# A list schedule on every queue from the out-projection's tenth tile to the ConvGLU's fourth unit

## Chip, cores and metric

The kernel runs on one core of one Trainium2 chip. Its time is the device time of one execution, in microseconds (us); the figures below are single executions and their median.

## What is computed

One hybrid decoder layer over 16 meta tokens and 512 tokens, with model width 2048, a hidden width of 5632 in the gated feed-forward part, all in fp32. Cut to its frame:

```python
h = jnp.concatenate([meta, x], axis=1)
n = rmsnorm(h, g_pre_mix)
z = n @ w_in
y_conv = short_conv_group(z[..., :CONV_COLS], conv_w)
y_rwkv = rwkv7_group(z[..., CONV_COLS:], ...)          # a scan over the tokens, 16 heads of 64
h = h + rmsnorm(jnp.concatenate([y_conv, y_rwkv], -1) @ w_out, g_post_mix)
gate, up = jnp.split(rmsnorm(h, g_pre_ffn) @ w_gate_up, 2, axis=-1)
h = h + rmsnorm((silu(causal_dwconv(gate, conv_ffn)) * up) @ w_down, g_post_ffn)
return h[:, N_META:]
```

## The kernel before

Features lie on the partitions and tokens along the free axis. KT = 16 blocks of 128 features make the model width. Tokens go in two halves of 258 and 256 columns (HY, lines 558 on; the two columns more are what the convolution looks back on). Every product of matrices is made of three fp32r matmuls: each operand is split in a high part (hi, cast by ScalarE, ACT) and a low part (lo, subtracted by VectorE, DVE), and hi by hi, hi by lo and lo by hi are summed in PSUM. In the rows `whi`, `wlo`, `H`, `O` and `tt` are split weights, `ahi` and `alo` are split activations, `R` and `raw` are the buffers into which weights land.

Work goes in three stages.

**Mixer (about 20 to 740 us).** The in-projection and the scan. Its instructions are not issued as written: class `Plan` (line 222) keeps them, estimates a duration for each (`time`) and a landing time for each DMA (`land`), and sorts each engine's queue by a list schedule with ranks (`order`, `run`). `give` (line 466) then issues them in that order under a manual schedule. A DMA's landing is taken as the issue, plus its bytes over 230 KB a us, plus LAND = 1.2 us, plus 2 us more if it has 4*NC = 68 partitions. A matmul of the rank FILL = 9 goes where nothing of a better rank is ready. The scan passes its matrices through DRAM: small tiles `Pi` go out to `d` (16 transfers of 32 partitions), a tile `tb` of 68 partitions goes out to `d`, and `AT` is read back from `d` in 32 transfers of 32 partitions. Its rounds are matmuls `st<-x,AT`, followed by `SUV` on DVE, ACT and GpSimd (POOL), before the next round's matmul.

**Out-projection and residual (about 740 to 1030 us).** Thirteen of the 16 output blocks of `w_out` (loop `for m in range(KT - 3)`, with `gemm`) are done for both token halves at a time. The last three are done by halves: first the three blocks' half 0 with the split weights kept in `tt0` to `tt2`, then the three blocks' half 1. Meanwhile `mixed` squares the outputs and sums the squares in `ss`, and copies them to `acc`. When half 0 is complete, `rms2` makes its norm (a ones-matmul into `psn`, then a few instructions on DVE and ACT that leave the factor `r1` in SBUF, in the tile `hxl`). `residual(i)` then takes blocks two at a time, eight pairs for each half: `xT` is loaded into one of three `q` buffers, DVE multiplies `acc` by `r1`, POOL adds `xT`, ACT and DVE split the sum to `ahi` and `alo`. The first units' matmuls (f = 0 and 1, half 0 and half 1, functions `halves2` and `standard`) read these.

PE's order here is the order of the code (a manual schedule for PE, line 1270), with `residual`'s steps started at fixed counts N1 = 9 and N2 = 5. The other queues are ordered by the framework's own scheduler.

**ConvGLU (to the end).** 44 units of 128 hidden features. Units f = 0 to 3 are plain products. From f = 4 on a unit is seven products of half size (`seven`), each one a "unit" of the list `units`, with sums of weights (DVE, POOL) and sums of activations (`X1` to `X4`, made once by `sums` and `last_sum`). After each group of four f, `down` adds the product with `w_down`. The list is issued with the products in order (line 1678). At the end come the second norm and the output.

Of the kernel before, what the change touches and what calls it, by code (L numbers as in the profile page):

```python
# [76 lines left out]
N4 = 2  # L77

# [117 lines left out]
class Pool:  # L196
# [3 lines left out]
    def tile(self, shape, dtype, **kw):  # L200
        if not self.plan.on:
            return self.real.tile(shape, dtype, **kw)
        t = Tile(self, shape, dtype, kw)
        return View(t, (), shape[0], t.ids)
# [17 lines left out]
class Plan:  # L222
# [243 lines left out]
    def give(self):  # L466
        self.on = False
        with self.tc.manual_schedule():
            for x in self.order():
                getattr(x["engine"], x["op"])(*x["args"], **x["kw"])  # L470
        self.kept = []


def hymba(tc, I, out, ysp=None):
# [60 lines left out]

    def split(x, hi, lo, scale=None):
# [18 lines left out]
    def rms(ss, r, m, q, psp, tag, pb=2, eps=None):  # L555
# [12 lines left out]
        V.tensor_tensor(out=r, in0=r, in1=q, op=ALU.mult)  # L568
# [621 lines left out]
    with tc.tile_pool(name="p2", bufs=1) as p2, tc.tile_pool(name="ps2", bufs=1, space=PSUM) as ps2:  # L1190
# [18 lines left out]
        def rms2(ss, r):  # L1209

            n = r.shape[-1]
            m = small(n)
            rms(ss, r, m, small(n), ps2, "d")
            return m

# [10 lines left out]
        def mixed(ps, m, i):  # L1226
# [3 lines left out]
            S.activation(out=sq[i], in_=x, func=AF.Square)  # L1230
# [4 lines left out]
        def residual(i, b12):  # L1235
# [3 lines left out]
            for m in range(0, KT, 2):  # L1239
                xr = two()[:, :, :b - a]  # L1240
# [10 lines left out]
        def act(b12, m, i):  # L1251

            if i and m < KT // 2:
                return [b12[:, m, p] for p in range(2)]
            return [x[:, i * HA:i * HA + 258] for x in hs[m]]
# [14 lines left out]
        with tc.manual_schedule(engines={mybir.EngineType.PE}):  # L1270
            last = []
            for n, m in enumerate(range(KT - 3, KT)):
                kw = p2.tile([128, KT // 4, 2, 512], F32R, name=f"tt{n}", bufs=1)
                keep = [(kw[:, ku, 0], kw[:, ku, 1]) for ku in range(KT // 4)]
                if n == 0:
                    ps = [ps2.tile([128, 512], F32, name="u", bufs=2) for _ in range(2)]
                else:
                    t = mp.tile([128, 2, 512], F32, name="mps")
                    ps = [t[:, i] for i in range(2)]
                run(gemm(I["w_out"][m], ys, half(ps, 0), into=keep))  # L1280
                mixed(ps, m, 0)
                last.append((ps, keep))
            n = 0
            res = iter(())
            for m, (ps, keep) in zip(range(KT - 3, KT), last):
                for _ in gemm(None, ys, half(ps, 1), kept=keep):
                    n += 1
                    if n == N1:
                        rms2([ss[0], sq[0]], r1[0])
                        res = residual(0, None)  # L1290
                    if n % 4 == 0:
                        next(res, None)
                mixed(ps, m, 1)
            run(res)


            H = KT // 2

            def block(n):
                return p2.tile([128, H, 2, 258], F32R, name=f"tt{n}", bufs=1)  # L1300

            b12 = block(2)
            rb = wide("rb")
            rw = [rb[:, i * HW:i * HW + 258] for i in range(2)]

            def load(src):
                raw = big("R", F32)
                SP.dma_start(raw, src)
                return raw

            def parted(raw, hi=None, lo=None):

                hi, lo = hi or [big("H")], lo or [big("O")]
                n = 1024 // len(hi)
                for i, x in enumerate(hi):
                    S.copy(x, raw[:, i * n:i * n + n])
                n = 1024 // len(lo)
                for i, x in enumerate(lo):
                    hn = len(hi) * n // 1024
                    hp = hi[0][:, i * n:i * n + n] if len(hi) == 1 else hi[i]  # L1320
                    V.tensor_tensor(out=x, in0=raw[:, i * n:i * n + n], in1=hp.bitcast(F32), op=ALU.subtract)

                def at(parts, c):
                    n = 1024 // len(parts)
                    return parts[c // n][:, c % n:c % n + 128]
                return lambda c: at(hi, c), lambda c: at(lo, c)

            def standard(outs, w, m0, x, first, last):

                for j in range(KT // 2):  # L1330
                    for pi, (p, q) in enumerate(((0, 0), (0, 1), (1, 0))):
                        for o, i, c in outs:
                            PE.matmul(o, w[p](128 * j), x(m0 + j, i)[q][:, c:258], start=(first and j == 0 and pi == 0),
                                      stop=(last and j == KT // 2 - 1 and pi == 2))
                    yield

            def x_of(m, i):
                return act(b12, m, i)
# [3 lines left out]
            hid = {}  # L1342

            def chain(f, zg, up, i0=0, i1=2, s=None):


                s = {} if s is None else s
                z3 = zg.rearrange("p (i t) -> p i t", i=2)[:, i0:i1]
                r3 = rb.rearrange("p (i t) -> p i t", i=2)[:, i0:i1]
                w = slice(256 * i0, 256 * i1)  # L1350

                def half3(x):
                    return x[:, w].rearrange("p (i t) -> p i t", t=256)

                def c0():
                    G.tensor_tensor(out=z3[:, :, :258], in0=z3[:, :, :258], in1=r3[:, :, :258], op=ALU.mult)

                def c1():
                    if "u" not in s:
                        s["u"] = wide()  # L1360
                    S.activation(out=half3(s["u"]), in_=z3[:, :, 0:256], func=AF.Copy, scale=pc("conv_ffn", f))

                def c2():
                    u3 = half3(s["u"])
                    for i in (1, 2):
                        V.scalar_tensor_tensor(out=u3, in0=z3[:, :, i:i + 256], scalar=pc("conv_ffn", i * NF + f),
                                               in1=u3, op0=ALU.mult, op1=ALU.add)

                def c3():
                    u = s["u"]  # L1370
                    S.activation(out=u[:, w], in_=u[:, w], func=AF.Silu)
                    if isinstance(up, list):
                        for i in range(2):
                            o = u[:, 256 * i:256 * i + 256]
                            V.tensor_tensor(out=o, in0=o, in1=up[i], op=ALU.mult)
                    else:
                        V.tensor_tensor(out=u[:, w], in0=u[:, w], in1=up[:, w], op=ALU.mult)

                def c4():
                    if f not in hid:  # L1380
                        if f % GF < 3:
                            hid[f] = [wp.tile([128, 512], F32R, name=n, bufs=3) for n in ("whi", "wlo")]
                        else:
                            hid[f] = [p2.tile([128, 2 * HW], F32R, name=n, bufs=1)[:, :SEQ] for n in ("hxh", "hxl")]
                    split(s["u"][:, w], *[x[:, w] for x in hid[f]])

                return [c0, c1, c2, c3, c4]

            def plain(f, ps, pu):
                zg = wide()  # L1390
                for i in range(2):
                    S.copy(zg[:, i * HW:i * HW + 258], ps[i])
                return chain(f, zg, pu)

            def first(f, n):
                t = mp.tile([128, 2, 512], F32, name="mps")
                u = ps2.tile([128, 512], F32, name="u", bufs=2)
# [463 lines left out]
```

## Time and profile before

| | us |
|---|---|
| three executions | 2421.02, 2416.26, 2418.2 |
| median | 2418.2 |
| the profiled execution | 2420.04 |
| its span on the core | 2417.9 |

| engine | busy us | share of the span | instructions |
|---|---|---|---|
| PE (matmul) | 2365.9 | 98% | 18546 |
| DVE | 1700.5 | 70% | 2274 |
| ACT | 1195.3 | 49% | 2343 |
| POOL | 670.8 | 28% | 753 |

Busy PE is not PE at its full rate: the profile also gives the clock that TensorE was granted, 1.0 being 2.4 GHz and 0.5 being 1.2 GHz. Over the whole span it is 0.994. A row such as "PE mps <- DVE alo: 6.0, 1, 6.0" says that PE, ahead of a matmul into `mps`, stood idle 6.0 us in total, once, until a DVE instruction that wrote `alo` released it.

### The profile page before, as it was taken

The numbers are of one execution on the slowest core, as the hardware profiler recorded it, in microseconds if no ns is written. First come the engines' busy times: TensorE is split into PE (matmuls) and PEld (weight loads), VectorE is DVE, ScalarE is ACT, GpSimd is POOL, SyncE is SP. The second block draws the span as 40 slices with busy tenths as digits, with TensorE's granted clock in tenths as the row PEclk, the third lists the DMA queues.
The fourth block names the chain that finished last, engine by engine and source line by source line (L and its number), as shares of the span: only waits on it lengthen the run. The fifth ranks groups of instructions, "written<-read, shape, count | busy, mean of one in ns | idle before, by whom it ended". The sixth has DMA issues, their size and how long they took to land.

```text
span 2417.9 us, 46262 instructions
## 1 busy us (share of the span) xinstructions
PE 2365.9 (98%) x18546; PEld 2253.1 (93%) x18546; DVE 1700.5 (70%) x2274; ACT 1195.3 (49%) x2343; POOL 670.8 (28%) x753
## 2 busy tenths in 40 slices
PE   7999999999999999999999999999999999999996
PEld 7999999999999999898999999999989898989896
DVE  7677888978754523885767777686868685859586
ACT  7756766666653533464434434343434252525254
POOL 2222747456350011531212111121212120202025
PEclk9999999999999999999999999999999999999998
DMA  5443333333433633523242424232424242323252
GB/s 180 146 140 107 93 89 88 103 106 87 136 98 92 201 92 110 175 66 97 82 127 79 131 79 123 81 121 77 126 68 140 70 131 79 119 83 108 94 194 73
DMA packets 130103, 265.53 MB, mean 110 GB/s; under 512 B 29888, under 2 KB 42944, under 8 KB 129888
## 3 DMA queue, kind: packets, MB, share of 16 engines
q1 hardware_dynamic: 129888, 262.57, 35.6%
q8 instruction: 146, 2.39, 0.4%
q14 instruction: 69, 0.57, 0.1%
HBM read 239.57 MB, written 22.95 MB: 109 GB/s over the span
## 4 chain that ended last, share of the span: by engine, by line
PE 90%; DVE 5%; DMA 2%; issue 1%; ACT 1%; POOL 0%; SPq 0%; DVEq 0%; ACTq 0%; POOLq 0%
PE mps L218 58%; PE u L218 16%; PE d L218 10%; PE st L218 4%; PE aux L218 2%; DVE acc L218 1%; DMA raw<-w_in_dram 1%; DVE raw L218 1%; DVE q L218 0%; DVE O L218 0%; DVE alo L218 0%; DVE tt L218 0%; DVE wlo L218 0%; DMA d<-tb 0%; DMA AT<-d 0%
## 5 line engine op out<-in xcount | busy, mean ns | idle before, releaser
L218 ACT CAST H<-R 128x1024 fp32r<-128x1024 f32 x373 | 391.9, 1051 | 454.8 <-PE u L218 177.6
L218 DVE TENSOR_TENSOR O<-R,H 128x1024 fp32r<-128x1024 f32 x373 | 488.9, 1311 | 109.0 <-ACT H L218 108.8
L218 PE MATMUL mps<-ahi,whi 128*128 128x264 f32 (+2 forms) x2048 | 411.2, 289 | 10.2 <-ACT whi L218 10.0
L218 PE MATMUL mps<-ahi,wlo 128*128 128x258 f32 (+2 forms) x2048 | 409.6, 288 | 1.6 <-DVE wlo L218 1.6
L218 PE MATMUL mps<-alo,whi 128*128 128x264 f32 (+2 forms) x2048 | 407.7, 287 | 0.2 <-DVE alo L218 0.2
L218 DVE TENSOR_TENSOR wlo<-raw,whi 128x512 fp32r<-128x512 f32 x289 | 209.1, 727 | 209.3 <-ACT whi L218 194.8
L218 PEld LDWEIGHTS mps<-ahi,whi 128*128 128x128 f32 x2048 | 313.5, 190 | 13.0 <-ACT whi L218 10.1
L218 PEld LDWEIGHTS mps<-ahi,wlo 128*128 128x128 f32 x2048 | 313.9, 190 | 4.3 <-DVE wlo L218 1.8
L218 PEld LDWEIGHTS mps<-alo,whi 128*128 128x128 f32 x2048 | 312.8, 190 | 2.2 <-DVE alo L218 0.5
L218 ACT CAST whi<-raw 128x512 fp32r<-128x512 f32 x289 | 178.3, 620 | 201.0 <-PE mps L218 154.4
L218 POOL TENSOR_TENSOR raw<-raw,rb 128x516 f32<-128x516 f32 (+1 forms) x45 | 92.5, 2057 | 627.8 <-DVE raw L218 613.1
L218 PE MATMUL mps<-tt,H 128*128 128x258 f32 x1968 | 263.3, 284 | 1.8 <-ACT q L218 1.8
L218 PE MATMUL mps<-alo,H 128*128 128x258 f32 x1032 | 255.2, 284 | 6.0 <-DVE alo L218 6.0
L218 PE MATMUL mps<-ahi,H 128*128 128x258 f32 x1032 | 255.1, 284 | 1.1 <-ACT q L218 1.1
L218 PEld LDWEIGHTS mps<-tt,H 128*128 128x128 f32 x1968 | 249.2, 190 | 2.0 <-ACT q L218 2.0
L218 POOL TENSOR_TENSOR R<-R 128x1024 f32<-128x1024 f32 x40 | 133.4, 3334 | 422.1 <-DVE R L218 422.1
L218 DVE TENSOR_TENSOR R<-R 128x1024 f32<-128x1024 f32 x120 | 208.9, 1741 | 1.1
L218 PEld LDWEIGHTS mps<-alo,H 128*128 128x128 f32 x1032 | 194.8, 190 | 6.7 <-DVE alo L218 6.2
L218 PEld LDWEIGHTS mps<-ahi,H 128*128 128x128 f32 x1032 | 195.4, 190 | 1.8 <-ACT q L218 1.3
L218 POOL TENSOR_SCALAR SUV<-VT 32x64 f32<-32x64 f32 x272 | 144.3, 531 | 137.0 <-PE st L218 109.7
L218 PE MATMUL mps<-ahi,O 128*128 128x258 f32 x1032 | 153.5, 284 | 0.0
L218 PE MATMUL mps<-tt,O 128*128 128x258 f32 x984 | 141.8, 283 | 0.0
(319 smaller groups left out, 4478.0 us busy)
## 6 DMA issues: line engine op xcount, KB each, us to landing
R<-w_gu_dram SPq DMA_DIRECT2D x176, 512.0 KB, 3.6
raw<-w_in_dram SPq DMA_DIRECT2D x208, 256.0 KB, 2.7
R<-w_down_dram SPq DMA_DIRECT2D x88, 512.0 KB, 4.4
raw<-w_out_dram SPq DMA_DIRECT2D x64, 256.0 KB, 2.7
l<-lo SPq DMA_DIRECT2D x24, 264.0 KB, 2.2
hsp<-acc SPq DMA_DIRECT2D x8, 512.0 KB
tt<-hsp SPq DMA_DIRECT2D x4, 1024.0 KB, 11.1
lo<-l SPq DMA_DIRECT2D x12, 264.0 KB, 3.5
```

Source lines behind the costliest of these rows:

```text
L218: return getattr(self.real, op)(*real, **{k: x.get() if isinstance(x, View) else x for k, x in kw.items()})
```

## The change

The plan that orders the mixer is used again, from the out-projection's block M0 = 10 to the ConvGLU's list entry K0 = 4, for all queues. Around that the code is changed as follows.

- Only the last two blocks of `w_out` are done by halves, not three.
- `rms1` writes the factor r1 into a PSUM tile, `r1p`. `residual` loads `xT` into a `raw` buffer (ring of three), multiplies by `r1p`, and adds on POOL and DVE in turn.
- Half 0's split blocks 0 to 7 get a block of their own, `b11` (tile `tt2`), from which `X11` is later read; half 1's go to the first columns of `hs`. `X4` then takes the place of those and needs no block.
- The sums of squares are added on DVE alone. `sums` and `last_sum` scale `h` on ACT (`normed`) and subtract pairs of blocks on DVE (`less`).
- `land` adds its 2 us also to transfers of C = 32 partitions, and Silu has a number in the table of ACT's function sets. Both bear on the mixer's order too, as all `d<-Pi` and `AT<-d` transfers have 32 partitions.
- All matmuls are the same ones, in another order.

```diff
-        return self.pipe + LAND + (2.0 if a.parts == 4 * NC else 0)
-    TABLE = {AF.Exp: 1, AF.Sigmoid: 2, AF.Tanh: 2, AF.Abs_reciprocal_sqrt: 3}
+        return self.pipe + LAND + (2.0 if a.parts in (C, 4 * NC) else 0)
+    TABLE = {AF.Exp: 1, AF.Sigmoid: 2, AF.Tanh: 2, AF.Abs_reciprocal_sqrt: 3, AF.Silu: 4}
...
+    def fill(g):
+        g = iter(g)
+        while True:
+            with plan.step(2, FILL):
+                try:
+                    next(g)
+                except StopIteration:
+                    return
+            yield
...
+        def rms1(i):
+            o = ps2.tile([128, 512], F32, name="r1p", tag="d", bufs=2)[:, :HY[i][1] - HY[i][0]]
+            with plan.step(0):
+                rms2([ss[i], sq[i]], r1[i], o)
+            r1[i] = o
...
-                xr = two()[:, :, :b - a]
+                xr = wide().rearrange("p (m t) -> p m t", m=2)[:, :, :b - a]
...
-                G.tensor_tensor(out=x, in0=x, in1=xr, op=ALU.add)
+                (G if m % 4 else V).tensor_tensor(out=x, in0=x, in1=xr, op=ALU.add)
                 for n in (m, m + 1):
-                    split(h[:, n, c:d], *act(b12, n, i), pc("g_ffn", n))
+                    with plan.step(1):
+                        split(h[:, n, c:d], *act(n, i), pc("g_ffn", n))
...
-        for m in range(KT - 3):
+        for m in range(KT - 2):
+            plan.on = m >= M0
...
-            run(gemm(I["w_out"][m], ys, [half(ps, i)[0] for i in range(2)]))
+            run(fill(gemm(I["w_out"][m], ys, [half(ps, i)[0] for i in range(2)])))
...
+        for k in range(-6, K0):
+            with plan.step(2, FILL):
+                if k >= 0:
+                    units[k][1]()
+            with plan.step(2):
+                if k > 0:
+                    units[k - 1][2]()
+                for e in ev.pop(k, []):
+                    e()
+                if 0 <= k + 2 < len(units):
+                    units[k + 2][0]()
+        plan.give()
```

Three places show what moves. The first is DVE's queue behind half 0's norm, before; `psn` is the sum of squares, `acc,hxl` the multiplication by r1, `tt<-R` the low parts of unit 1's weights, `alo` those of the activations:

```order
L218 TENSOR_SCALAR q<-psn 128x258
L218 TENSOR_TENSOR q<-q 128x258
L218 TENSOR_SCALAR q<-q 128x258
L218 TENSOR_TENSOR hxl<-hxl,q 128x258
L218 TENSOR_TENSOR acc<-acc,hxl 128x2x258 x8
L218 TENSOR_TENSOR tt_13691<-R,tt_13691 128x1024 x2
L218 TENSOR_TENSOR tt_13700<-R,tt_13700 128x1024 x2
L218 SCALAR_TENSOR_TENSOR alo_11511<-acc,par,ahi_11510 128x258
```

The same place of DVE's queue in the changed kernel, where `tt_13584` is the own block for half 0 and `acc,raw` the addition of `xT`:

```order
L220 TENSOR_SCALAR q<-psn 128x258
L220 TENSOR_TENSOR q<-q 128x258
L220 TENSOR_SCALAR q<-q 128x258
L220 TENSOR_TENSOR r1p<-hxl,q 128x258
L220 TENSOR_TENSOR acc<-acc,r1p 128x2x258 x4
L220 TENSOR_TENSOR acc<-acc,raw 128x2x258
L220 SCALAR_TENSOR_TENSOR tt_13584<-acc,par,tt_13584 128x258 x4
L220 TENSOR_TENSOR acc<-acc,raw 128x2x258
L220 TENSOR_TENSOR acc<-acc,r1p 128x2x258
L220 SCALAR_TENSOR_TENSOR tt_13584<-acc,par,tt_13584 128x258
```

Behind four multiplications and one addition come the first four low parts; the weights' low parts (`tt<-R`) have moved behind half 1's.

The second is ACT's queue where the first products of unit 4 end, before; `q<-mps` copies a finished product out of PSUM, `tt<-raw` is the high part of a late sum:

```order
L218 CAST tt_14713<-raw 128x2x258 x3
L218 CAST H<-R 128x1024
L218 COPY raw<-mps 128x258 x2
L218 CAST H<-R 128x1024
L218 COPY q<-mps 128x258
L218 ACTIVATE raw<-raw,par 128x512
L218 CAST tt_14713<-raw 128x258
L218 CAST H<-R 128x1024
L218 COPY q<-mps 128x258
L218 CAST tt_14713<-raw 128x258
L218 CAST H<-R 128x1024
L218 COPY q<-mps 128x258
```

In the changed kernel the late sums are `ahi_...<-raw`:

```order
L220 COPY raw<-mps 128x258 x2
L220 ACTIVATE q<-acc,par 128x258 x2
L220 CAST H<-R 128x1024
L220 CAST ahi_13883<-raw 128x258
L220 CAST ahi_13888<-raw 128x258
L220 CAST H<-R 128x1024
L220 COPY q<-mps 128x258
L220 ACTIVATE raw<-raw,par 128x512
L220 ACTIVATE q<-acc,par 128x258
L220 CAST H<-R 128x1024
L220 CAST ahi_13832<-raw 128x258
L220 COPY q<-mps 128x258
```

The first copy stands behind two casts of sums that were subtracted earlier; of the later two, one has a cast of a late sum ahead of it instead of both.

The third is SyncE's queue, SP, in the mixer, at the scan's third set of matrices, before; `d_...<-tb` sends them out and `AT<-d` reads them back:

```order
L218 DMA d_7045<-tb 68x1024
L218 DMA ysp<-sg 128x514
L218 DMA raw<-w_in_dram 128x512
L218 DMA sg<-l_1606 128x528
L218 DMA raw<-w_in_dram 128x512
L218 DMA AT<-d_7045 32x9x32 x4
L218 DMA AT<-d_7045 32x8x32 x2
L218 DMA raw<-w_in_dram 128x512
L218 DMA AT<-d_7045 32x8x32 x2
```

And in the changed kernel:

```order
L220 DMA ysp<-sg 128x514
L220 DMA raw<-w_in_dram 128x512 x2
L220 DMA sg<-l_1606 128x528
L220 DMA d_7113<-tb 68x1024
L220 DMA raw<-w_in_dram 128x512 x2
L220 DMA AT<-d_7113 32x9x32 x4
L220 DMA AT<-d_7113 32x8x32 x4
```

The store of y and the load of `sg` no longer stand between the sending and the reading back, and the eight readings go in one row.

## Rows read from the trace of the kernel before

**Rows 1.** The page's parts 1 and 4: engines, and the chain that ended last.

```profile
PE 2365.9 (98%) x18546; PEld 2253.1 (93%) x18546; DVE 1700.5 (70%) x2274; ACT 1195.3 (49%) x2343; POOL 670.8 (28%) x753
...
PE 90%; DVE 5%; DMA 2%; issue 1%; ACT 1%; POOL 0%; SPq 0%; DVEq 0%; ACTq 0%; POOLq 0%
```

**Rows 2.** PE's waits, 650 to 1250 us: us in total, times, longest.

```profile
PE mps L218 <- DVE alo L218: 6.0, 1, 6.0
PE mps L218 <- ACT q L218: 2.9, 2, 1.8
PE u L218 <- DVE raw L218: 0.4, 1, 0.4
```

**Rows 3.** Windows: us, each engine's busy time (instructions), PEclk, DMA share, GB/s.

```profile
960.00:970.00 10.00, 10.00 (x85) 10.00 (x85) 0.69 (x1) 2.06 (x6) 1.65 (x2) 1.00 0.01 2
...
980.00:990.00 10.00, 8.00 (x67) 7.79 (x65) 10.00 (x7) 6.88 (x15) 8.82 (x7) 1.00 0.49 114
990.00:1000.00 10.00, 6.00 (x31) 5.78 (x32) 8.75 (x16) 1.93 (x6) 5.23 (x3) 0.66 0.71 257
...
1100.00:1110.00 10.00, 7.12 (x47) 6.71 (x47) 8.24 (x14) 6.41 (x11) 0.00 (x0) 0.86 0.46 150
1110.00:1120.00 10.00, 10.00 (x69) 9.41 (x69) 5.39 (x8) 3.99 (x6) 2.15 (x1) 0.97 0.66 218
```

**Rows 4.** The chain that ended last, 980 to 1000 us: start, us, what.

```profile
979.58 7.90 DVE acc L218 x5
...
988.54 5.00 DVE tt L218 x3
993.55 0.41 DVE alo L218
```

**Rows 5.** DVE's instructions by shape, 972 to 994 us: busy us, mean ns, idle before.

```profile
L218 DVE TENSOR_TENSOR acc<-acc,hxl 128x516 f32<-128x516 f32 x8 | 10.9, 1433 | 0.0
L218 DVE TENSOR_TENSOR tt<-R,tt 128x1024 fp32r<-128x1024 f32 x4 | 6.1, 1592 | 0.0
L218 DVE SCALAR_TENSOR_TENSOR alo<-acc,par,ahi 128x258 fp32r<-128x258 f32 x2 | 0.9, 477 | 0.0
L218 DVE TENSOR_SCALAR q<-psn 128x258 f32<-128x258 f32 x1 | 0.4, 428 | 12.8 <-PE psn L218 12.8
```

**Rows 6.** DVE and POOL by shape, 972 to 1107 us.

```profile
L218 DVE SCALAR_TENSOR_TENSOR alo<-acc,par,ahi 128x258 fp32r<-128x258 f32 x24 | 13.7, 635 | 0.4 <-ACT ahi L218 0.3
...
L218 POOL TENSOR_TENSOR acc<-acc,q 128x516 f32<-128x516 f32 x8 | 14.8, 1865 | 18.1 <-DVE acc L218 12.1 <-DMA q<-xT_dram 5.8
```

**Rows 7.** DVE by shape, 100 to 740 us: a product read from PSUM.

```profile
L218 DVE TENSOR_TENSOR z<-mps,rstd 128x528 f32<-128x528 f32 x23 | 16.1, 702 | 1.8 <-PE mps L218 1.5
```

**Rows 8.** DVE of tile R, 972 to 1107 us: ns min/median/max, first and last start.

```profile
L218 DVE TENSOR_TENSOR O<-R,H x13: 1210/1224/2310, 1038.8 to 1106.1; 128x1024 fp32r<-128x1024 f32 x13
```

**Rows 9.** DMA issues, 972 to 1107 us: KB each, median us to landing.

```profile
q<-xT_dram SPq DMA_DIRECT2D x8, 258.0 KB, 3.7
```

**Rows 10.** ACT in order of time, 1099 to 1107 us: start, us.

```profile
1104.69 0.41 ACT L218 CAST tt<-raw 128x258 fp32r<-128x258 f32 x1 [3.33 <-DVE raw L218]
...
1105.95 0.37 ACT L218 COPY q<-mps 128x258 f32<-128x258 f32 x1
```

**Rows 11.** PE's waits in the mixer, 100 to 745 us.

```profile
PE st L218 <- DMA AT<-d: 4.9, 3, 2.1
PE st L218 <- DVE SUV L218: 2.9, 3, 1.2
```

**Rows 12.** Tile AT there: ns min/median/max of its matmuls; landing of its transfers.

```profile
L218 PE MATMUL st<-x,AT x136: 217/273/324, 214.6 to 737.3; 128*128 128x64 f32 x136
...
DMA to landing us min/median/max: 1.9/2.4/3.9
```

**Rows 13.** Windows in the mixer around one such wait.

```profile
490.00:500.00 10.00, 7.87 (x66) 7.32 (x66) 5.87 (x9) 6.21 (x17) 4.56 (x10) 0.98 0.57 145
500.00:510.00 10.00, 10.00 (x82) 9.55 (x83) 4.16 (x8) 6.02 (x18) 6.42 (x10) 0.85 0.18 53
```

More of the change, by code (lines that the diff above doesn't have):

```diff
@@ L470, in give @@
                 getattr(x["engine"], x["op"])(*x["args"], **x["kw"])
+        for x in self.kept:
+            for a in [x["out"]] + x["ins"]:
+                if isinstance(a, View):
+                    a.tile.uses = []
         self.kept = []
@@ L1187, in hymba @@
         plan.give()
-    with tc.tile_pool(name="p2", bufs=1) as p2, tc.tile_pool(name="ps2", bufs=1, space=PSUM) as ps2:
+    with ExitStack() as ctx2:
+        p2, ps2 = pool(ctx2, "p2", 1), pool(ctx2, "ps2", 1, "psum")
         WB = {"R": 5, "H": 3, "O": 3}
@@ L1229, in mixed @@
             sq[i] = ss[i] if m == 0 else small(b - a)
-            S.activation(out=sq[i], in_=x, func=AF.Square)
+            with plan.step(0 if m >= KT - 2 else 2):
+                S.activation(out=sq[i], in_=x, func=AF.Square)
             if 0 < m < KT - 1:
@@ new lines, in hymba, with block @@
+        H = KT // 2
+        def block(n):
+            return p2.tile([128, H, 2, 258], F32R, name=f"tt{n}", bufs=1)
+        b11 = block(2)
+        last = []
+        for n, m in enumerate(range(KT - 2, KT)):
+            kw = p2.tile([128, KT // 4, 2, 512], F32R, name=f"tt{n}", bufs=1)
+            keep = [(kw[:, ku, 0], kw[:, ku, 1]) for ku in range(KT // 4)]
+            if n == 0:
+                ps = [ps2.tile([128, 512], F32, name="u", bufs=2) for _ in range(2)]
+            else:
+                t = mp.tile([128, 2, 512], F32, name="mps")
+                ps = [t[:, i] for i in range(2)]
+            run(fill(gemm(I["w_out"][m], ys, half(ps, 0), into=keep)))
+            mixed(ps, m, 0)
+            last.append((ps, keep))
@@ new lines, in hymba, with load @@
+        n = 0
+        res = iter(())
+        for m, (ps, keep) in zip(range(KT - 2, KT), last):
+            for _ in fill(gemm(None, ys, half(ps, 1), kept=keep)):
+                n += 1
+                if n == N1:
+                    rms1(0)
+                    res = residual(0)
+                if n % 4 == 0:
+                    next(res, None)
+            mixed(ps, m, 1)
+        run(res)
+        rb = wide("rb")
+        rw = [rb[:, i * HW:i * HW + 258] for i in range(2)]
+        def load(src):
+            raw = big("R", F32)
+            SP.dma_start(raw, src)
+            return raw
@@ new lines, in plain, with first, halves2 @@
+        def plain(f, ps, pu):
+            zg = wide()
+            for i in range(2):
+                S.copy(zg[:, i * HW:i * HW + 258], ps[i])
+            return chain(f, zg, pu)
+        def first(f, n):
+            t = mp.tile([128, 2, 512], F32, name="mps")
+            u = ps2.tile([128, 512], F32, name="u", bufs=2)
+            return [t[:, i, :258] for i in range(2)], [u[:, i * 256:i * 256 + 256] for i in range(2)]
+        def halves2(ff, w, i):
+            for b in range(4):
+                o = (ff[b // 2][i], i, 2 * (b // 2))
+                yield from standard([o], w[b], H * (b % 2), x_of, b % 2 == 0, b % 2 == 1)
@@ new lines, in beside @@
+        def beside():
+            yield from residual(1)
+            sb = [wide() for _ in range(2)]
+            for j in range(H):
+                for n in (2 * j, 2 * j + 1):
+                    x = sb[j % 2] if n < 4 and n % 2 == 0 else two().rearrange("p a b -> p (a b)")
+                    S.activation(out=x[:, :TY], in_=h[:, n], func=AF.Square)
+                    if x is not sb[j % 2]:
+                        V.tensor_tensor(out=sb[j % 2][:, :TY], in0=sb[j % 2][:, :TY], in1=x[:, :TY], op=ALU.add)
+                yield
+            norms.append(sb)
@@ new lines, in last_sum @@
+        def last_sum(X2, j, n):
+            x = normed(two()[:, :n], H + j, 0)
+            t = wide().rearrange("p (a b) -> p a b", a=2)[:, :n]
+            V.tensor_tensor(out=t, in0=X2[:, j:j + n, 0].bitcast(F32), in1=X2[:, j:j + n, 1].bitcast(F32), op=ALU.add)
+            less(t, x, t)
+            for i in range(n):
+                split(t[:, i], *[y[:, :258] for y in hs[j + i]])
+        norms = []
+        res = iter(())
+        side = iter(())
+        n = 0
+        for i in range(2):
+            for f in ((0, 1), (1, 0))[i]:
+                for _ in fill(halves2(ff[f], (w0, w1)[f], i)):
+                    n += 1
+                    if n == N2:
+                        rms1(1)
+                        res = beside()
+                    if n % 2 == 0:
+                        next(res, None)
@@ new lines, in down_pe, with add_up @@
+        def down_pe(g, m, pd, w, a, b, ii):
+            for i in ii:
+                xs_ = hid[g * GF + i]
+                for pi, (p, q) in enumerate(((0, 0), (0, 1), (1, 0))):
+                    PE.matmul(pd, w[p](512 * (m % 2) + 128 * i), xs_[q][:, a:b], start=(i == 0 and pi == 0),
+                              stop=(i == GF - 1 and pi == 2))
+        def add_up(g, m, pd, a, b):
+            if g == 0:
+                S.copy(acc[:, m, a:b], pd)
+            else:
+                V.tensor_tensor(out=acc[:, m, a:b], in0=acc[:, m, a:b], in1=pd, op=ALU.add)
```

603 lines of the change are left out of this document (256 added, 347 removed).

## The prediction

> **What bounds the kernel now.** I read the page first. PE is busy 98% of the span, and 90% of the chain that ended last is PE [rows 1]. The matmuls are the same in the changed kernel, so only the time in which PE stands idle or runs at the lower clock can move. I therefore read PE's waits in two stretches, the one that the change rewrites and the mixer, which it reorders by a number in the plan, and then the granted clock around each wait.
>
> From 650 to 1250 us PE waits four times, 9.3 us in all [rows 2]. The long one is 6.0 us for the first low part of an activation, `alo`. The windows show what comes with it: 85 matmuls go into 10 us at the full rate, but 67 from 980 to 990 us and 31 from 990 to 1000 us, at a granted clock of 0.66 [rows 3]. A mean of 0.66 is 6.8 us at the lower level (1.2 GHz), of which about 2 us lie in the wait and 4 behind it; PE worked some 4 us at half rate and lost about 2. I call this loss A: 6.0 + 2.0 = 8.0 us. The chain says whose work it is: DVE's multiplications `acc` by r1, then four `tt` (the low parts of unit 1's weights), then at 993.55 us the first `alo` [rows 4]. Eight multiplications took 10.9 us and four `tt` 6.1 [rows 5], so r1 was ready at 993.55 - 17.0 = 976.5 us. The low part that PE needed stood behind 17 us of DVE work of which about a quarter was needed for it.
>
> Loss B is 0.4 us (`raw`). Loss C is two waits, 2.9 us, for the copy `q<-mps` on ACT [rows 2], and a clock of 0.86 and 0.97 in the windows behind, which is 2.8 + 0.6 us at the lower level and so 1.7 us lost [rows 3]; together 4.6. ACT's order of time shows why: the copy at 1105.95 us stands behind a cast `tt<-raw`, and ACT had been idle 3.33 us for DVE's `raw` [rows 10].
>
> In the mixer PE waits three times for `AT<-d`, 4.9 us in all, and three times for DVE's `SUV`, 2.9 [rows 11]. The longest `AT` wait also lowers the clock: 0.98 and 0.85 over two windows are 3.4 us at the lower level, 1.7 lost [rows 13]. The other two waits for `AT` leave no more than 2.8 us between them.
>
> **The change part by part.** The sum is made against the profiled execution, 2420.04 us, which is 1.8 above the median of 2418.2 and inside the three executions' spread. I carry the difference over to the median.
>
> Loss A. In the new order DVE does four multiplications, one addition and one low part ahead of the first `alo` that PE needs. A multiplication beside POOL's additions took 1433 ns [rows 5]; DVE's product with one operand in PSUM took 702 [rows 7], and with r1 in PSUM I take that. An addition on DVE has no row; its size is that of the product, and I take 0.69, at most 1.43. Before, some 119 matmuls of the out-projection stood behind `psn`, 14 us at 85 in 10; PE ran dry at 988.0, so `psn` ended near 974.0 and r1 came 2.5 us later. Now the first low part comes at 2.5 + 4 x 0.70 + 0.69 + 0.48 = 6.5 us, at most 2.5 + 5 x 1.43 + 0.64 = 10.3. The cover has shrunk, because two blocks instead of three are done by halves: 87 matmuls, 10.2 us. So the 6.0 us go, by either price.
>
> What is late next is DVE as a whole. From half 0's `psn` to the ConvGLU norm's sums its queue holds 16 multiplications, 8 additions, 32 low parts of activations, 5 of weights, 14 additions of squares and 8 small instructions. With 0.70, 0.69, 0.48 [rows 5], 1.22 [rows 8], 0.69 and 0.40 that is 11.2 + 5.5 + 15.4 + 6.1 + 9.7 + 3.2 = 51.1 us. PE has 381 matmuls there, 44.8 us, and about 0.7 for the second `psn`. DVE is longer by 5.6 us. Some of its last items need not be done by then in full, and PE need not run dry in one piece; with low parts at the 635 ns that they took beside POOL [rows 6] it is 5 us worse. I take 3.5 us of new waits, in pieces too short for the clock (each low window in these rows stands behind a wait of 1.8 us or more), with 1 and 7 as ends. Loss A becomes 3.5: gain 4.5.
>
> Here a rule bears on the multiplications. They took 1433 ns while POOL added beside them. The Trainium skill (SBUF — State Buffer, section "SBUF: two separate sides") says that a DVE instruction with two inputs in SBUF and a GpSimd instruction that reads SBUF take turns at a shared pair of ports, one blocked for the whole of the other. By that rule r1 in PSUM frees the multiplications, and the trace's 635 against 477 ns for `alo` agrees; but DVE's new additions and its low parts would still be held up by POOL's remaining additions. With the dearer low parts, as the rule has it, loss A keeps 8.5 us instead of 3.5 and the time would be 2410.7; without it, 2405.7.
>
> The loads. `xT` goes through a ring of three `raw` buffers, each held for a landing of 3.7 us [rows 9], the multiplication and an addition of up to 1.87 on POOL [rows 6], about 6 us. Thirteen reloads over three buffers are 13 x 6 / 3 = 26 us, inside PE's 45. It is hidden; it would decide only from some 10 us a buffer.
>
> Losses B and C. The sums are made earlier, by scaling on ACT and subtracting on DVE, and ACT's first copy `q<-mps` has no late sum between its release and itself; the second still has one. One wait of the two would be 1.4 us; half of that, 0.7, is kept. Gain 5.0 - 0.7 = 4.3, with 2 and 5 as ends. ACT's scalings (some thirty, at the 0.37 of a copy [rows 10], 11 us) lie in a stage where ACT was busy 6.9 us in 10 at most [rows 3]; they cost nothing unless they stand ahead of a copy again.
>
> The mixer. All 32 readings of `AT` and 16 writings of `d` are now planned to land 2 us later. `AT` landed in 1.9 to 3.9 us [rows 12], against 1.2 plus its bytes in the plan before, so the correction is in the right direction, and the longest wait for it was 2.1 us [rows 11]. The eight readings also go in one row. I let 4.9 + 1.7 = 6.6 us go. But the plan changes the order of everything behind the first `AT`, and a new order has waits of its own that the plan did not foresee; the nearest row is what the old one had, 2.9 us for `SUV`, so I charge that once more. Gain 6.6 - 2.9 = 3.7, from -3 (all gain lost and as much again as `SUV`) to +9.5 (the old `SUV` waits go too).
>
> Sum: 4.5 + 4.3 + 3.7 = 12.5 us, so 2407.5 for an execution like the profiled one, and 2418.2 - 12.5 = **2405.7 us** against the median.
>
> **The rivals.**
>
> *All waits go.* DVE's work is hidden, and the plan fits the mixer: 8.0 + 5.0 + 6.6 + 2.9 = 22.5 us, 2395.7. For it: DVE overlaps instructions, so 51.1 may be too much. Against it: DVE would have to be without a wait in a stretch where its work is as long as PE's.
>
> *The residual stretch still waits.* DVE with low parts at 635 ns and additions at 1433 needs 51.1 + 5.1 + 5.9 = 62 us against 45.5, and the waits are again about the 8.0 that loss A was, if half of the difference falls on PE; the mixer's reorder eats what it gives. Only 4.3 is left: 2413.9. For it: the 31 matmuls and DVE's 10.00 of 10 us at 980 to 990 [rows 3] show DVE with no reserve. That the change doesn't do what it says is the extreme of this case: multiplications from PSUM that are no faster, so that `alo` comes as late as before.
>
> *The scan loses its beat: slower.* The reorder moves the matmuls `st<-x,AT` and the `SUV` behind them among other work on DVE, ACT and POOL. There are 136 of them [rows 12], each waits for the one before through `SUV`, and only a few waits show now. If one in eight has to wait the 1.2 us of the longest `SUV` wait [rows 11], that is 17 x 1.2 = 20.4 us, against 8.8 from A, B and C: 11.6 slower, 2429.8. It decides the sign from 8.8 / 1.2, 7 to 8 such waits; a loss beyond 0.2% takes 11 or 12. For it: the plan's number moves 48 transfers at once. Against it: the old order came from the same plan with a worse number and had three.
>
> **How the numbers follow.** About 0.2%, 4.8 us, is what a measurement of this kernel can tell from no change; the bounds are 2413.4 and 2423.0. The forecast (gain 6 to 18) has 0.53, all waits gone 0.12, the residual stretch still waiting 0.22, the scan out of beat 0.13. Faster: 0.53 + 0.12 and a small part of the third, 0.02, is 0.67. Slower: most of the last, 0.12. The same: 0.21. The range runs from 2397, near the case of all waits gone, to 2421, which leaves out most of the slower case and little else.
>
> **What would show it.** In the changed kernel's profile: PE's wait for `alo` no longer 6.0 us in one piece and no window near 990 us with a clock of 0.66; multiplications with `r1p` near 0.70; short waits for DVE between half 0's `psn` and the ConvGLU norm, 1 to 7 us in all; at most one wait for `q<-mps`; no wait above 0.5 us for `AT<-d`, and waits for `SUV` under 6 us in all. Wrong would be: multiplications still near 1.4 us, a wait on `xT`, or mixer waits above the 7.8 of `AT` and `SUV` together now.

## The result: 23.9 us faster, and a third of it from a place that the prediction had ruled out

| | before | after |
|---|---|---|
| median us | 2420.62 (5 runs, 2416.26 to 2421.36) | 2396.72 (5 runs, 2395.36 to 2397.63) |
| profiled execution us, span | 2420.04, 2417.9 | 2395.92, 2394.1 |
| ratio of after to before | | 0.9905, 95% interval 0.9891 to 0.9920 |

The sign was right, and so were the places that the forecast named, but 23.9 us were gained where 12.5 were forecast, and 2396.7 lies at the very end of its range (2397). The first lines of the page of the changed kernel:

```profile
span 2394.1 us, 46253 instructions
...
PE 2354.7 (98%) x18546; PEld 2249.2 (94%) x18546; DVE 1699.1 (71%) x2277; ACT 1202.7 (50%) x2364; POOL 632.0 (26%) x734
```

PE has the same 18546 matmuls, but its busy time has fallen by 11.2 us from [rows 1]. A low clock that goes gives back some of that, and so far the forecast holds. The rest can't come from waits.

PE's waits in the changed kernel, 650 to 1250 us (us in total, times, longest), where [rows 2] had 9.3 us:

```profile
PE mps L220 <- DVE tt L220: 1.3, 1, 1.3
PE mps L220 <- DVE alo L220: 0.5, 1, 0.5
PE mps L220 <- ACT ahi L220: 0.4, 1, 0.4
```

The waits in the mixer, 100 to 745 us, where [rows 11] had 7.8 us for `AT` and DVE's `SUV`:

```profile
PE st L220 <- POOL s L220: 0.8, 1, 0.8
PE mps L220 <- ACT whi L220: 0.5, 1, 0.5
PE st L220 <- DVE SUV L220: 0.5, 1, 0.5
PE aux L220 <- DVE t L220: 0.3, 1, 0.3
```

No wait for `AT` is left. And four windows (us, busy time and instructions of PE, its weight loads, DVE, ACT, POOL, then PEclk, DMA share, GB/s):

```profile
500.00:510.00 10.00, 9.48 (x85) 8.96 (x84) 7.68 (x12) 8.27 (x23) 5.76 (x10) 1.00 0.27 80
980.00:990.00 10.00, 8.61 (x67) 7.95 (x66) 9.63 (x20) 6.64 (x15) 2.53 (x2) 1.00 0.41 106
990.00:1000.00 10.00, 8.94 (x70) 8.28 (x68) 10.00 (x21) 6.50 (x15) 3.69 (x3) 1.00 0.82 264
...
1090.00:1100.00 10.00, 10.00 (x85) 9.96 (x84) 6.70 (x11) 3.69 (x5) 2.15 (x1) 1.00 0.68 218
```

The clock is 1.00 in all of them, where it was 0.85, 0.66 and 0.86 in the windows of the three losses [rows 3, 13].

Idle PE from its first matmul to its last adds up to 23.7 us before and 10.9 after. I set the two traces beside each other by the count of matmuls done. After the mixer the changed kernel is some 6 us ahead and after unit 4's first products 17.6. From there to the tail, where the order of the products is the same and no engine is waited for in either, it gains another 6.7 us, evenly. That part sits in the spacing, the distance from start to start, of the 512-column matmuls with `w_down`. Three in a row, before and after (start, us):

```profile
1372.41 0.40 PE L218 MATMUL d<-whi,H 128*128 128x512 f32 x1
1372.64 0.40 PE L218 MATMUL d<-wlo,H 128*128 128x512 f32 x1
1372.88 0.39 PE L218 MATMUL d<-whi,O 128*128 128x512 f32 x1
```

```profile
1353.99 0.39 PE L220 MATMUL d<-whi,H 128*128 128x512 f32 x1
1354.22 0.39 PE L220 MATMUL d<-wlo,H 128*128 128x512 f32 x1
1354.44 0.39 PE L220 MATMUL d<-whi,O 128*128 128x512 f32 x1
```

The durations tell the same with more digits. Tile `d` from 1300 to 1500 us (ns min/median/max, first and last start), before and after:

```profile
L218 PE MATMUL d<-whi,H x27: 392/394/398, 1372.4 to 1498.9; 128*128 128x512 f32 x27
L218 PE MATMUL d<-wlo,H x27: 388/393/397, 1372.6 to 1499.1; 128*128 128x512 f32 x27
```

```profile
L220 PE MATMUL d<-whi,H x36: 389/389/389, 1354.0 to 1493.3; 128*128 128x512 f32 x36
L220 PE MATMUL d<-wlo,H x36: 389/389/390, 1354.2 to 1493.6; 128*128 128x512 f32 x36
```

Over all 1920 such matmuls the mean distance from one start to the next is 230.8 ns before and 226.9 after: 3.83 x 1920 = 7.4 us. The 6500 or so matmuls of 258 columns in the same stage stand at 120.3 and 120.2. So the two profiled executions add up: 12.8 us of idle PE, 3.9 of clock (half of the time that PE worked at the lower level, 5.4 before and 1.5 after) and 7.4 of spacing are 24.1, and the spans differ by 23.8. The same PSUM banks are used, the two of `d` in the other order. What also differs is the SBUF address of the split weights: the changed code uses its tiles in another order, so the pool places H at 150880 instead of 204576 and O at 163168 instead of 216864 (bytes within a partition).

### The profile page after: what moved, and what is told of

Read it like the earlier page. It is cut to its first block, busy times and chain, and to the rows that moved or that the text cites. A ratio compares the mean times of both kernels' runs of the same rounds, so it can differ in the third digit from the quotient of the medians.

```text
span 2394.1 us, 46253 instructions
## 1 busy us (share of the span) xinstructions
PE 2354.7 (98%) x18546; PEld 2249.2 (94%) x18546; DVE 1699.1 (71%) x2277; ACT 1202.7 (50%) x2364; POOL 632.0 (26%) x734
## 4 chain that ended last, share of the span: by engine, by line
PE 56%; DVE 2%; issue 0%; ACT 0%; POOL 0%; ACTq 0%; DVEq 0%; POOLq 0%
PE mps L220 30%; PE u L220 16%; PE d L220 10%; DVE acc L220 1%; DVE alo L220 0%; DVE raw L220 0%; PE psn L220 0%; DVE q L220 0%; POOL raw L220 0%; ACT q L220 0%; DVE O L220 0%; DVE tt L220 0%; ACT raw L220 0%; ACT acc L220 0%; DVE r1p L220 0%
## 5 line engine op out<-in xcount | busy, mean ns | idle before, releaser
L220 PE MATMUL mps<-ahi,whi 128*128 128x264 f32 (+2 forms) x2080 | 416.7, 288 | 10.5 <-ACT whi L220 10.5
L220 PE MATMUL mps<-alo,whi 128*128 128x264 f32 (+2 forms) x2080 | 416.0, 288 | 0.7 <-DVE alo L220 0.7
L220 PE MATMUL mps<-ahi,wlo 128*128 128x264 f32 (+2 forms) x2080 | 412.7, 287 | 1.6 <-DVE wlo L220 1.6
L220 DVE TENSOR_TENSOR wlo<-raw,whi 128x512 fp32r<-128x512 f32 x293 | 221.1, 758 | 208.1 <-ACT whi L220 189.0
L220 PEld LDWEIGHTS mps<-ahi,whi 128*128 128x128 f32 x2080 | 318.1, 189 | 13.2 <-ACT whi L220 10.7
L220 PEld LDWEIGHTS mps<-alo,whi 128*128 128x128 f32 x2080 | 317.6, 189 | 3.5 <-DVE alo L220 1.1
L220 POOL TENSOR_SCALAR SUV<-VT 32x64 f32<-32x64 f32 x272 | 138.0, 508 | 159.3 <-PE st L220 132.6
```

The lines of the kernel that those rows point to most:

```text
L220: return getattr(self.real, op)(*real, **{k: x.get() if isinstance(x, View) else x for k, x in kw.items()})
```

## Experiments

Each comparison is against runs of the kernel before on the same chip. In the diffs "pad" is a tile that nothing uses. The spacing is always the mean of the 1920 matmuls.

**The addresses of the kernel after, in the kernel before.** My theory after the result: 7 to 9 us are placement alone. The tiles of the last stages are named once in another order ahead of their use, so that they get the changed kernel's addresses; no instruction moves, and the PSUM banks stay those of before.

```diff
+        for name, shape, dt, n in (("hxh", [128, 2 * HW], F32, 1), ("acc", [128, KT, TY], F32, 1), ("q", [128, 2, 258], F32, 3),
+                                   ("R", [128, 1024], F32, 5), ("H", [128, 1024], F32R, 3), ("O", [128, 1024], F32R, 3),
...
+            p2.tile(shape, dt, name=name, bufs=n)
         h = p2.tile([128, KT, TY], F32, name="acc", bufs=1)
```

> The kernel before, its instructions and their order unmoved, with its SBUF tiles of the last stages at the addresses of the changed kernel (R at 130400, H at 150880, O at 163168, hxh, acc, hxl and rb likewise). Placement theory: the 512-column matmuls go from 230.8 to about 226.9 ns a piece as in the changed kernel and the time falls by 6.5 to 9 us with the waits as before. Rival (the spacing is set by what other engines do beside the matmuls): spacing stays at 230.8, time within 1 us.

Measured: 2410.89 against 2419.79 us, ratio 0.9963 (0.9951 to 0.9976), 8.9 us. The spacing is 226.7 ns. Tile `d` in this run:

```profile
L218 PE MATMUL d<-whi,H x30: 389/389/389, 1371.2 to 1499.6; 128*128 128x512 f32 x30
L218 PE MATMUL d<-wlo,H x30: 389/389/389, 1371.4 to 1499.8; 128*128 128x512 f32 x30
```

The waits of the kernel before are all still there (6.1 us for `alo`, 1.1 and 1.8 for `q`). So placement alone, with the old order of instructions and of PSUM banks, is shown to be worth 5.8 to 11.9 us by the runs; 4.1 ns in 1920 matmuls are 7.9 of it.

**64 bytes ahead of the weight buffers of the kernel before.** I first took the phase of 128 bytes to be what counts.

```diff
             rb = wide("rb")
+            p2.tile([128, 16], F32, name="pad", bufs=1)
```

> The kernel before, with an unused tile of 64 bytes per partition ahead of the weight buffers R, H and O, so that they start at 96 instead of 32 modulo 128, as in the changed kernel; no instruction is moved. Placement theory: the 512-column matmuls of w_down go from a spacing of about 231 ns to about 227, and the time falls by about 1728 x 4 ns = 6.5 us. Rival (the spacing comes from the order of the other engines' work, or from the changed activations' tiles): spacing stays near 231 and the time stays within 1 us.

Measured: 2422.23 against 2418.61, ratio 1.0014 (1.0005 to 1.0023), with a spacing of 232.0 ns. Both sides missed: the spacing moved, so addresses count, but upward, so the phase of 128 bytes is not the rule.

**64 bytes in the changed kernel,** ahead of R and again behind O.

```diff
+            name = self.kw.get("name")
+            if name in ("R", "tt0") and name not in self.pool.padded:
+                self.pool.padded.append(name)
+                self.pool.real.tile([128, 16], F32, name="pad" + name, bufs=1)
             self.real = self.pool.real.tile(self.shape, self.dtype, **self.kw)
```

> The changed kernel with 64 unused bytes ahead of R and 64 behind O, so that R, H and O start at 32 modulo 128 as before; no instruction is moved. Placement theory: the spacing of the 512-column matmuls rises from 227 to about 231 ns and the time by about 6.5 us. Rival: no change.

Measured: 2413.07 against 2418.61, ratio 0.9978 (0.9969 to 0.9987): with no instruction moved, 16 us of the changed kernel's gain are gone. The spacing is 233.3 ns, which is 12.3 us over 1920 matmuls, and the 258-column matmuls stand at 120.7 instead of 120.2, another 3.1. Tile `d`:

```profile
L225 PE MATMUL d<-whi,H x36: 393/396/398, 1358.2 to 1499.6; 128*128 128x512 f32 x36
```

This run is also the nearest to the sum that I had made. Its spacings are worse than those of before; the difference is 2.5 x 1920 = 4.8 and about 0.45 x 6500 = 2.9 us. Without that it would stand near 2405, some 13 us under the kernel before; that figure is an estimate.

**Other shifts: 32, 128 and 192 bytes** ahead of R in the changed kernel.

```diff
+            if self.kw.get("name") == "R" and not self.pool.padded:
+                self.pool.padded = True
+                self.pool.real.tile([128, 8], F32, name="pad", bufs=1)
             self.real = self.pool.real.tile(self.shape, self.dtype, **self.kw)
```

> The changed kernel with 32 unused bytes ahead of R, so that H and O start at 0 modulo 128 and every tile behind them moves by 32; no instruction is moved. If the spacing follows the addresses' distance modulo 256, it is another value than 226.9 and 233.3 ns for the 512-column matmuls; if only the parity of 64 bytes counts, one of these two.

> The same with 128 bytes, so that H and O start at 96 modulo 128 as in the changed kernel, at 224 instead of 96 modulo 256. If a phase of 128 bytes counts, the spacing stays at 226.9 ns and the time at 2397; if 256 or more, it goes to 229 to 233 and the time up by 4 to 11 us.

> The same with 192 bytes, H and O at 32 modulo 128 as in the run with 64. If a phase of 128 bytes counts, the spacing is 233 ns and the time 2411 to 2414; if 256, some other value.

| shift of H and O | ratio to before | us | spacing, 512 columns | 258 columns |
|---|---|---|---|---|
| none (the changed kernel) | 0.9905 | 2396.72 | 226.9 | 120.2 |
| 32 | 0.9960 (0.9947 to 0.9974) | 2409.01 | 233.2 | 120.1 |
| 64 (and 64 behind O) | 0.9978 (0.9969 to 0.9987) | 2413.07 | 233.3 | 120.7 |
| 128 | 0.9964 (0.9952 to 0.9976) | 2409.99 | 232.4 | 120.5 |
| 192 | 0.9954 (0.9939 to 0.9970) | 2407.91 | 231.2 | 120.5 |

128 bytes ruled out the phase of 128, and with it the parity of 64, which that shift keeps too. The 32 bytes gave 233.2, one of the two values that parity would have given, so that run by itself rules nothing out. Nor is the distance modulo 256 enough: H stands at the same phase to the moving tile `whi` in the changed kernel (226.9) and in the kernel before with 64 bytes (232.0).

What is shown is that addresses alone move the spacing, and that the effect is the same every time: each of the distances is the same within 1 ns in the changed kernel and in the three runs below that leave its addresses in this stage (old landing times, r1 in SBUF, all additions on POOL). Which addresses count is not shown. I sorted the distances by the pair of addresses of the moving tile and of the next matmul's weights. Within a pair they vary by 1.1 ns (standard deviation), over all by 3.5, and the means of the pairs go from 224.1 to 240.8. But every pair occurs in one placement only, and the weights of the matmul itself sort them just as well. The changed kernel even has the same matmul into `u`, with the same SBUF addresses and PSUM bank and between neighbours with the same addresses, at two distances: 236 ns in the first block of each group's `down` (1100.5 us and nine times more) and 227 in a later block (1133.1 us and nine times more). The durations around these two places:

```profile
L220 PE MATMUL u<-whi,H x4: 389/396/397, 1099.8 to 1102.5; 128*128 128x512 f32 x4
```

```profile
L220 PE MATMUL u<-whi,H x4: 389/389/389, 1133.1 to 1135.8; 128*128 128x512 f32 x4
```

So the pair is not the whole rule, and the mechanism stays open: other engines' tiles moved with the weights, and a clash with their reads was not tested. The place that the changed kernel happens to have is the best of the seven.

**The landing times alone, in the kernel before.**

```diff
-        return self.pipe + LAND + (2.0 if a.parts == 4 * NC else 0)
+        return self.pipe + LAND + (2.0 if a.parts in (C, 4 * NC) else 0)
-    TABLE = {AF.Exp: 1, AF.Sigmoid: 2, AF.Tanh: 2, AF.Abs_reciprocal_sqrt: 3}
+    TABLE = {AF.Exp: 1, AF.Sigmoid: 2, AF.Tanh: 2, AF.Abs_reciprocal_sqrt: 3, AF.Silu: 4}
```

> The kernel before with the plan's landing times of the changed kernel (2 us more for transfers of 32 partitions, a number for Silu) and nothing else. Theory: the whole of the mixer's gain, waits from 8.9 to about 3 us and no low clock near 500 us, 6 to 8 us faster. Rival (the mixer gains from something else in the change): under 2 us.

Measured: 2415.18 against 2418.61, ratio 0.9985 (0.9977 to 0.9994): 1.5 to 5.6 us. PE's longest waits in the mixer are now

```profile
PE st L218 <- POOL s L218: 1.1, 1, 1.1
PE aux L218 <- ACT lo L218: 1.0, 2, 0.6
```

and the low clock near 500 us is gone. In the profiled executions this kernel is 6.9 us ahead at the end, 5.6 of it at 980 us. The rest is no gain of the mixer: the two waits for `q` near 1100 us are still there (2.8 us), but in this execution no low clock follows them. The mechanism is as expected; the time is under the 6 to 8 that I gave it.

**The old landing times in the changed kernel** (the same edit, the other way, without the table).

> The changed kernel with the old landing times in the plan, so that the mixer has its old order. Theory: the mixer's waits and its low clock come back; from the run of the kernel before with the new landing times, 3 to 7 us slower than the changed kernel, 2400 to 2404. Rival (the mixer gains nothing): 2397.

Measured: 2402.75, ratio 0.9930 (0.9918 to 0.9943): 0.0025 of the time, or 6 us, above the changed kernel, whose interval (0.9891 to 0.9920) this one just touches. The waits are back:

```profile
PE st L220 <- DMA AT<-d: 5.0, 3, 2.2
PE st L220 <- DVE SUV L220: 2.3, 3, 1.1
```

From both sides, the mixer's new order is worth 3.5 to 6 us, give or take 2 to 5.

**r1 in PSUM alone, in the kernel before.** The queues keep their order.

```diff
+        def rms1(i):
+            o = ps2.tile([128, 512], F32, name="r1p", tag="d", bufs=2)[:, :HY[i][1] - HY[i][0]]
+            rms2([ss[i], sq[i]], r1[i], o)
+            r1[i] = o
...
-                        rms2([ss[0], sq[0]], r1[0])
+                        rms1(0)
```

> The kernel before with the factor r1 in PSUM and nothing else; the queues keep their order. If SBUF reads of POOL's additions are what lengthens the multiplications, they fall from 1433 to about 700 ns, the first low part comes 5.8 us earlier, PE's 6.0 us wait is almost gone and with it the low clock: about 8 us faster. Rival (the order of the queues makes the wait): multiplications stay above 1.2 us and the time falls by less than 2 us.

Measured: 2415.89 against 2418.61, ratio 0.9989 (0.9980 to 0.9998), 2.7 us (0.5 to 4.8) of the 8. DVE by shape, 972 to 998 us (busy us, mean ns, idle before), beside [rows 5]:

```profile
L218 DVE TENSOR_TENSOR tt<-R,tt 128x1024 fp32r<-128x1024 f32 x4 | 7.9, 2046 | 0.0
L218 DVE SCALAR_TENSOR_TENSOR alo<-acc,par,ahi 128x258 fp32r<-128x258 f32 x7 | 5.3, 823 | 0.0
L218 DVE TENSOR_TENSOR acc<-acc,r1p 128x516 f32<-128x516 f32 x8 | 4.9, 685 | 0.0
```

The multiplications fell from 1433 to 685 ns, which I had taken as 700. But POOL's eight additions now run beside what comes next: the `tt` went from 1592 to 2046 and the `alo` from 477 to 823. Counted from r1, the first `alo` ended 3.2 us earlier, not 5.8 (it took 1.49 us itself); PE's wait fell from 6.0 to 2.8 us, and a window with a clock of 0.83 remained. That is the Trainium skill's exclusive lock (SBUF — State Buffer, section "SBUF: two separate sides"), and this trace agrees with it: the instruction with one input in PSUM escapes, and those with two in SBUF pay.

**r1 in SBUF, in the changed kernel.**

```diff
-            o = ps2.tile([128, 512], F32, name="r1p", tag="d", bufs=2)[:, :HY[i][1] - HY[i][0]]
             with plan.step(0):
-                rms2([ss[i], sq[i]], r1[i], o)
-            r1[i] = o
+                rms2([ss[i], sq[i]], r1[i])
```

> The changed kernel with r1 left in SBUF (the list schedule plans with it). Theory (the order of the queue did most of it, PSUM some): multiplications back at 1.0 to 1.4 us, PE's waits between the two norms up by 2 to 5 us from 2.4. Rival (POOL's additions are few now, so SBUF costs nothing): within 1 us of the changed kernel.

Measured: 2413.76, ratio 0.9976 (0.9967 to 0.9986), 17 us worse than the changed kernel. The number that I gave for the multiplications was wrong, and so the reason: they take 688 ns here too. In this run the last three multiplications of half 0 stand behind four low parts, at 989.96 us. The likely reason, read from the plan's code and not tested, is that the plan reckons with the lock: while POOL adds, it puts a DVE instruction with two SBUF inputs aside for another. POOL's addition and ACT's cast follow only then. The chain of this run, 985 to 996 us (start, us, what):

```profile
990.73 2.27 POOL acc L220
...
993.02 0.52 ACT tt L220
```

PE's longest waits from 650 to 1250 us, and two windows:

```profile
PE mps L220 <- ACT tt L220: 4.7, 1, 4.7
PE mps L220 <- ACT ahi L220: 3.7, 1, 3.7
```

```profile
990.00:1000.00 10.00, 6.02 (x29) 5.73 (x30) 8.29 (x16) 4.17 (x9) 4.14 (x3) 0.66 0.44 133
...
1010.00:1020.00 10.00, 6.01 (x30) 5.50 (x29) 9.77 (x17) 7.86 (x16) 1.42 (x1) 0.66 0.53 187
```

Each long wait again takes the clock with it. With the list schedule, PSUM is worth far more than the 2.7 us that it has alone; that it leaves the schedule free to put the multiplications first is how I explain it.

**All additions of `xT` on POOL, in the changed kernel.**

```diff
-                (G if m % 4 else V).tensor_tensor(out=x, in0=x, in1=xr, op=ALU.add)
+                G.tensor_tensor(out=x, in0=x, in1=xr, op=ALU.add)
```

> The changed kernel with all sixteen additions of xT on POOL, none on DVE. Theory (DVE's total is what PE waits for, and POOL's reads stretch DVE's low parts): low parts of activations go from 0.49 to 0.6 or more, POOL's additions become the late step, waits in the residual stretch rise by 2 to 6 us. Rival (DVE is relieved of 5.5 us and PE waits less): 1 to 2 us faster.

Measured: 2397.90, ratio 0.9911 (0.9896 to 0.9926), the same as the changed kernel within what can be told. DVE by shape, 968 to 1016 us, first in the changed kernel and then in this one:

```profile
L220 DVE SCALAR_TENSOR_TENSOR alo<-acc,par,ahi 128x258 fp32r<-128x258 f32 x24 | 10.5, 491 | 0.6 <-ACT ahi L220 0.6
...
L220 DVE TENSOR_TENSOR acc<-acc,r1p 128x516 f32<-128x516 f32 x8 | 5.1, 684 | 0.0
...
L220 DVE TENSOR_TENSOR acc<-acc,raw 128x516 f32<-128x516 f32 x4 | 2.8, 688 | 0.0
```

```profile
L220 DVE SCALAR_TENSOR_TENSOR alo<-acc,par,ahi 128x258 fp32r<-128x258 f32 x24 | 14.3, 658 | 0.0
```

The low parts do grow as expected, from 491 to 658 ns, 24 x 0.17 = 4.0 us and 1.6 more for the eight into the own block (567 to 767). But DVE is rid of eight additions of 0.69, 5.5 us. The two cancel on DVE. PE waits 2.6 us where the changed kernel's three waits add up to 2.2, but in one piece, and the clock falls behind it, where the changed kernel had 1.00:

```profile
PE mps L220 <- DVE tt L220: 2.6, 1, 2.6
```

```profile
990.00:1000.00 10.00, 10.00 (x73) 10.00 (x73) 10.00 (x20) 4.28 (x10) 4.62 (x4) 0.83 0.40 129
```

I estimate that at some 2 us, 0.4 of waiting and half of the 3.4 us at the lower clock, which these runs cannot tell from nothing. The split of the additions between the engines is not what made the kernel faster by more than that.

**Three parts without the schedule, in the kernel before:** the landing times, r1 in PSUM and the addresses, by the edits above together.

> The kernel before with three of the changed kernel's parts and without its list schedule: new landing times, r1 in PSUM, the changed kernel's addresses. If the parts add up as measured alone (3 to 6, 3 and 9 us) it is 15 to 18 us faster than before, 2401 to 2404, and what the changed kernel is faster still, 4 to 8 us, is the list schedule's and the recast code's own. Rival (the schedule is worth next to nothing beside these): 2397.

Measured: 2401.00 against 2419.08, ratio 0.9929 (0.9917 to 0.9942), 17 to 18 us. Alone the three gave 3.4, 2.7 and 8.9, together 15.0. What is left to the list schedule and the recast code in the out-projection and the first units is 4 to 6 us: the medians are 4.3 apart, the ratios 0.0024, and the intervals of the ratios overlap a little. In this run PE still waits 4.1 us for `alo` and 0.8 for `q`, with a clock of 0.83 in two neighbouring windows.

## Why the prediction came out as it did

*Loss A.* Forecast to fall from 8.0 to 3.5 us; it fell to 2.4, with the waits that are too short for the list above, and no low clock stands behind it. The working held up in its prices: multiplications 684 ns (taken as 700), additions 688 (690), low parts 491 (480), 567 for the eight into the own block. The first low part was ready 6.9 us behind half 0's `psn` (worked out as 6.5), before PE needed it, and DVE was late as a whole, as forecast, by a little less. The dearer low parts of the other branch (635 ns, 2410.7 us) did not come, but the longest wait, 1.3 us, is for one of them: the sixth, which took 1.14 us beside an addition on POOL. What the sum did not say is how little r1 in PSUM does by itself: the run with that alone shows that the delay passes on to the next instructions. The list schedule and the recast code together turn it into time; which of the two is not shown.

*Losses B and C.* Forecast 4.3 of 5.0; all 5.0 went. The second copy with a late sum ahead of it did not hold PE up. The 1.7 us for the clock in them does not come every time: in the run with the landing times alone the same waits had none behind them.

*The loads.* Said to be hidden from PE by a wide margin. PE never waits for them, but POOL does, 16.8 us from 968 to 1016 us, 8.0 at the longest. From 984 to 1000 us the chain that ended last goes through DVE and not through the loads. Whether they are far from deciding was not tested.

*The mixer.* Forecast 3.7, charged with 2.9 us of new waits for `SUV`. No new waits came: idle time there fell from 8.9 to 2.8 us, and the low clock went, 6.1 + 1.7 = 7.8 us of which some 1.5 are lost again to a low clock in the first 30 us. By the runs it is worth 3.5 to 6. The allowance of 2.9 was too large by the traces; by the lower of the two runs it was about right. The rival in which the scan loses its beat did not show at all.

*What was not in the sum.* The step that failed is the first one, and it put the term at nothing without a reason: "The matmuls are the same in the changed kernel, so only the time in which PE stands idle or runs at the lower clock can move." The spacing of equal matmuls moved as well, by 3.8 ns in 1920 of them, because a recast program places its tiles elsewhere. The run with the addresses alone puts it at 8.9 us, the spacing at 7.4. This part is luck: nobody chose the place, and the padded runs show that others cost 11 to 16 us of the gain, with a spacing worse than before the change. Had the placement been like that of the 64-byte run, with all of the change's own gains, I should have seen 5.5 us instead of 23.9.

So the gain divides into 7 to 9 us of placement, 3.5 to 6 of the mixer's landing times, and the rest, 7 to 9 by the runs (2.7 for r1, 4 to 6 for schedule and recast code), from the residual stretch and the first units, where 8.8 had been forecast. In the profiled executions that stretch gave 10.7 us, from 980 us to the end of unit 4's first products. The rival in which all waits go gives nearly the measured time, 2395.7, and is wrong all the same: 10.9 us of idle PE are left. Tail and start gave nothing: the tail's waits grew from 2.4 to 3.2 us, and the profiled execution has one low window in the first 30 us that the one before has not.

No run beat the changed kernel.

## What to carry to other kernels

Where one engine is busy 98% of the time, compare the distance from start to start of its commonest instructions before and after, not only its waits: a change that touches no matmul can move each of them by a few ns. Before crediting a rewrite with its gain, run the old code with the new addresses and the new code with a small shift; both leave every instruction where it is. And where two engines hold each other up over SBUF, as DVE and POOL do here, look at what stands next in the queue before moving one operand to PSUM: here the delay passed to those instructions.

## What the runs showed of the hardware

- The time from one matmul to the next depends on where tiles lie in SBUF. For 512 columns its mean went from 226.7 to 233.3 ns with the addresses alone, single distances repeat within 1 ns from execution to execution, and by position they go from 224.1 to 240.8 ns. By which operands, the runs do not show. A shift of the weight buffers by 32 to 192 bytes cost 11 to 16 us in this kernel.
- A DVE product with one operand in PSUM took 685 ns beside POOL's additions, with both in SBUF 1433; the delay then went to the next instructions with two SBUF inputs.
- Waits for a transfer vary from one execution to the next: the longest `AT` wait was 2.1 us in the profiled execution of before and 3.7 in that of the run with r1 in PSUM alone, whose mixer is the same. With 6.8 instead of 3.4 us at the lower clock near 500 us, that mixer ends 3.7 us later.
- The clock does not fall behind every such wait: near 1107 us, behind a wait of 1.8 us for `q`, it stood at 0.86 before and at 1.00 in the run with the landing times alone.
